# Requests for weights and residual rows kept in written order on SyncE's queue

## The chip, the cores and the metric

The kernel runs on one core of one Trainium2 chip. A core has five engines that work side by side, each through its own instructions in order: TensorE (PE in the profile; PEld are its weight loads), VectorE (DVE), ScalarE (ACT), GpSimd (POOL) and SyncE (SP). SyncE computes nothing here. It issues nearly all the transfers, and while an instruction at the head of its queue waits for a semaphore, all behind it wait too. Transfers run on 16 DMA engines. The metric is device time in microseconds; 1191.49 is the median of three runs before.

## The reference

Two decoder layers over 1024 tokens of width 1024. Each layer projects its input once into a main part, memory queries and two gates; makes a main result and a cross-attention into 256 memory tokens; gates both; multiplies them by W_out; adds the scaled input and normalises.

```python
def mixer_sublayer(x, mem, w_in, w_mem_kv, w_out, main_fn):
    h = x @ w_in
    u_main = h[..., :D_MAIN]
    q_mem = h[..., D_MAIN:D_MIX]
    g_main = h[..., D_MIX:D_MIX + D_MAIN]
    g_mem = h[..., D_MIX + D_MAIN:]
    y_main = main_fn(u_main)
    y_mem = memory_attention(q_mem, mem, w_mem_kv)
    y = jnp.concatenate([y_main * jax.nn.silu(g_main), y_mem * jax.nn.silu(g_mem)], axis=-1)
    return y @ w_out
...
        x = layer_norm(ALPHA * x + y, ln_g[layer], ln_b[layer])
```

The main result of layer 0 is a causal pooling; that of layer 1 is a causal attention of 16 heads of width 64, with a forget bias that is added to the logits. Its keys and values come from one projection of layer 0's output.

## The kernel before

Every product is made of two or three matmuls of narrower numbers: a weight or an activation is split into a high and a low half, and the halves are multiplied crosswise.

*Slabs.* `slab` projects onto 128 columns: two pieces of weights of 128 x 512, 48 matmuls of 512 columns, two accumulators, each evacuated when it is full. In layer 1 the slabs of keys (`k_units`), queries (`q_units`), values (`v_units`) and gates (`gate_units`) are generators. The attention sweep (`fox`) goes through 16 heads, two to a pair, and 8 tiles of 128 queries to a head, from the longest row of keys to the shortest, and between its own matmuls it pumps matmuls out of a list of such generators (`Fill`). The slabs of pair p+1 are filled in while pair p is attended to: k, then q, then v, and with pairs 0, 2, 4 and 7 gate slabs as well. So the order of TensorE is written out by hand there (`tc.manual_schedule`).

*How a slab of the fill gets its weights.* While `low[0]` is set, both pieces come in one transfer of 512 KB into a tile of the tag "B" (ten buffers), line 332. Then GpSimd scales a piece (L176), makes its high half (L193) and its low half (L178). The generator yields after the request and after each split, and `Fill.pump` takes these three steps of the slab that is second in the list: the request as soon as the slab ahead of it has become the first, the splits when fewer than 30 and 16 of its 48 matmuls are left. The head pair's k slab is stepped at set tiles instead (i = 2, 5 and 6 of the second head).

*Other work on SyncE in the sweep.* `turn` issues a transpose of a tile's probabilities (L1081), with the values' matmuls (L1090) six tiles later; `move` copies halves of a finished k or q slab to other partitions (L909), three transfers of which the third overwrites what the first read; `forget_rows` loads the bias of a head (L1009); `values_of` transposes a v slab (L823); results are stored (L1119) and late gates load and store them again (L1126, L1131). GpSimd also makes the masks of the diagonal (L1002), which VectorE reads with the logits (L1028).

*W_out.* `OutProj` holds 24 pieces of W_out to a layer. In layer 1, `fetch_two` asks for them two at a time during the last head pair and after it (L557), `split` takes them in order some tiles later. `rest` then goes through four blocks of 256 rows and three chunks of W_out's rows: it loads gated results (L634), splits them, multiplies (L599) and, after a block's last chunk, calls `norm`, which loads the residual rows (L655), adds (L659), normalises and stores (L673).

*What sets the order of the rest.* Outside what is written by hand, a planner orders each engine's instructions by their place in the program and by when it thinks that they are ready and their buffer is free. An instruction without inputs, such as a load of weights, can so be issued long before the place at which it is written. `tc.keep_in_program_order` gives an instruction an order-only edge to the instruction written just before it on the same engine; it is not issued before that one. It adds no wait for that one's end, and later instructions are not held behind it by it.

Of the kernel before, what the change touches and what calls it, by code (L numbers as in the profile page):

```python
# [18 lines left out]
P = 128  # L19
# [53 lines left out]
def run(units):  # L73
    for _ in units:
        pass
# [3 lines left out]
def trunk_kernel(ctx, tc, x, xT, memT, win, wk, wv0, wv, wmk, wmv, wout, poolw, pscale, lng, lnb, bforget, out):  # L79
# [5 lines left out]
    nc = tc.nc  # L85
# [18 lines left out]
    def sb(shape, tag, bufs, dt=F32, where=None):  # L104
        return (where or pool).tile(shape, dt, tag=tag, name=nm(tag), bufs=bufs)

    def ps(shape, tag, bufs):
        return psum.tile(shape, F32, tag=tag, name=nm(tag), bufs=bufs)

    def G(shape=(P, S), dt=F32):  # L110
        return sb(list(shape), "G", 4, dt)

    def T(shape=(P, S), dt=F32R):
        return sb(list(shape), "T", 6, dt)
# [10 lines left out]
    def tiny(n, dt=F32):  # L125
        return small.tile([P, n], dt, tag=f"s{n}{dt}", name=nm("s"), bufs=4 if n < 12 else 2)
# [53 lines left out]
    def parts_of(make, shape):  # L180
        return Split(make(shape), make([shape[0], 2] + list(shape[1:]), BF16))
# [7 lines left out]
    def three(a, b):  # L189
        return (a.hi, b.hi), (a.top, b.lo), (a.lo, b.hi if isinstance(a, Wide) else b.top)  # L190
# [18 lines left out]
    def split_w(src_dram, shape, sc=None, r=None, pin=lambda ins: ins):  # L209
        if r is None:  # L210
            r = raw(shape)
            nc.sync.dma_start(r, src_dram)
        if sc is not None:
            to = half_of(wt, shape)
            if low[0]:
                gp_scaled_hi_lo(to, r, sc)
            else:
                scaled_hi_lo(to, r, sc, pin)
            return to
        to = parts_of(wt, shape)  # L220
        (gp_hi_lo if low[0] else hi_lo)(to, r)
        return to
# [102 lines left out]
    def slab(pieces_dram, X, evac, banks=("pj", 2), g=0):  # L325

        arrived = isinstance(pieces_dram, list)
        sc = sws[g] if isinstance(X, Half) else None
        both = (None, None)
        if low[0]:  # L330
            wide = roomy[0]([P, 2, 4, P])
            nc.sync.dma_start(wide, pieces_dram.rearrange("c p k m -> p c k m"))
            both = wide[:, 0], wide[:, 1]
            yield 0
        ws = list(pieces_dram) if arrived else [split_w(pieces_dram[0], [P, 4, P], sc, both[0])]
        if low[0]:
            yield 0
            ws.append(split_w(pieces_dram[1], [P, 4, P], sc, both[1]))
            yield 0
        accs = {}  # L340
        high, low_top = (0,), (1, 2)
        if sc is not None:
            order = [(n, pc, (0, 1, 2)) for n in range(2) for pc in range(2)]
        elif arrived:
            order = [(n, pc, part) for pc in range(2) for n, part in ((0, high), (1, high), (1, low_top), (0, low_top))]
        else:
            order = [(0, pc, part) for part in (high, low_top) for pc in range(2)]
            order += [(1, pc, part) for part in (low_top, high) for pc in range(2)]
        seen = {0: 0, 1: 0}
        for n, pc, part in order:  # L350
            if len(ws) <= pc:
                ws.append(split_w(pieces_dram[pc], [P, 4, P], sc, both[pc]))
            if n not in accs:
                accs[n] = ps([P, NH], *banks)
            for i in part:
                a, b = three(ws[pc], X)[i]
                for k in range(4):
                    seen[n] += 1
                    nc.tensor.matmul(  # L359
                        accs[n], a[:, k, :], b[:, pc * 4 + k, n * NH : (n + 1) * NH],  # L360
                        start=seen[n] == 1, stop=seen[n] == 3 * KT,
                    )
                    if seeing[0]:
                        seeing[1] += 1
                        if seeing[1] % 8 == 0:
                            look_ahead()
                    if seen[n] == 3 * KT:
                        evac(slice(n * NH, (n + 1) * NH), accs[n])
                    yield NH
# [174 lines left out]
    class OutProj:  # L544
# [8 lines left out]
        def fetch_two(self, land):  # L553

            n = self.n + len(self.raws)
            for j, to in enumerate(land):
                nc.sync.dma_start(to, wout[self.l, n // 2 % 2, 2 * self.KKS[n // 4] + j])  # L557
                self.raws.append(to)

        def fetch(self, upto):  # L560
# [54 lines left out]
        def rest(self, resid, X, dst):  # L615
            order = [(sp, c) for sp in range(ST // 2) for c in (2, 0, 1)]
            accs, splits, gb = {}, [24], []
            if self.accs:
                accs[0], order[:6], splits = self.accs, [(0, 0), (1, 2), (0, 1), (1, 0), (1, 1)], [16, 24]
            if X is not None:  # L620
                self.split(splits.pop())

            def loads():

                for v in (lng, lnb):
                    t = sb([P, D], "P", 4)
                    nc.sync.dma_start(t, v[self.l].partition_broadcast(P))
                    gb.append(t)

            for sp, c in order:  # L630
                if c == 2:
                    accs[sp] = self.open((("T", 2), ("T", 2), ("L", 3), ("O", 1))) if 0 in accs and sp == 1 else self.open()
                src, ys = T([P, 4, 2 * P], F32), parts_of(T, [P, 4, 2 * P])
                nc.sync.dma_start(src, self.yd[c, :, :, sp * 2 * P : (sp + 1) * 2 * P])  # L634
                hi_lo(ys, src)
                if splits:
                    self.split(splits.pop(0), X is None)
                if not gb and not splits:
                    loads()
                run(self.products(accs[sp], c, ys, X is None and sp == ST // 2 - 1 and c == 1))  # L640
                if X is not None and (sp, c) == (0, 0):
                    scale_of_norm(gb)
                if X is not None and c == 0 and sp:
                    scales_of_weights(sp - 1)
                if X is not None and c == 0 and sp in (1, 2):
                    keep(sp - 1)
                if c == 1:
                    norm(sp, accs.pop(sp), gb, resid, X, dst)

    def norm(sp, accs, gb, resid, X, dst):  # L650
        for a in range(2):
            s = 2 * sp + a
            rows = slice(s * P, (s + 1) * P)
            z = G()
            nc.sync.dma_start(z, resid[rows, :])  # L655
            stats = tiny(12)
            for nh in range(2):
                zn = z[:, nh * NH : (nh + 1) * NH]
                nc.vector.scalar_tensor_tensor(zn, zn, ALPHA, accs[a][nh], ALU.mult, ALU.add)  # L659
                nc.vector.bn_stats(stats[:, 6 * nh : 6 * nh + 6], zn)  # L660
            mv, v, sd, r, t = tiny(2), tiny(1), tiny(1), tiny(1), tiny(1)
            nc.vector.bn_aggr(mv, stats.rearrange("p (a b) -> p a b", a=2))
            nc.vector.tensor_scalar(v, mv[:, 1:2], LN_EPS, None, ALU.add)
            nc.scalar.activation(sd, v, AF.Sqrt)
            nc.vector.reciprocal(r, sd)
            nc.vector.tensor_scalar(t, r, r, v, ALU.mult, ALU.mult)
            nc.vector.tensor_scalar(t, t, -0.5, 1.5, ALU.mult, ALU.add)
            nc.vector.tensor_tensor(r, r, t, ALU.mult)
            for cols in (slice(0, NH), slice(NH, D)) if s == ST - 1 else (slice(0, D),):
                nc.vector.scalar_tensor_tensor(z[:, cols], z[:, cols], mv[:, 0:1], gb[0][:, cols], ALU.subtract, ALU.mult)  # L670
            for cols in (slice(0, NH), slice(NH, D)) if s == ST - 1 else (slice(0, D),):
                nc.vector.scalar_tensor_tensor(z[:, cols], z[:, cols], r, gb[1][:, cols], ALU.mult, ALU.add)  # L672
                nc.sync.dma_start(dst[rows, cols], z[:, cols])  # L673
            if X is not None:
                two = Half(*(lines[0][:, 9 + 2 * (s % 3) + e, :] for e in range(2)))
                scaled_hi_lo(two, z, sx)
                for to, half in ((X.hi, two.hi), (X.lo, two.lo)):
                    nc.sync.dma_start_transpose(to[:, :, rows], half)
# [5 lines left out]
    X = parts_of(stream, [P, KT, S])  # L684
# [110 lines left out]
    X = X1  # L795
# [501 lines left out]
```

## Time and profile before

| | us |
|---|---|
| median of 3 runs (lowest, highest) | 1191.49 (1191.08, 1192.35) |
| the profiled execution | 1193.08 |
| its span | 1191.4 |
| TensorE busy | 1166.9 |
| VectorE busy | 782.7 |
| ScalarE busy | 684.8 |
| GpSimd busy | 286.0 |

The span runs from the first to the last instruction; the execution's own time holds a little more. Rows of a timeline give the start and the duration in microseconds, the engine (SPq is SyncE's queue, where the duration is that of issuing), the line, the operation, what is written and read, and a count where equal instructions are merged; in brackets stand the idle time of the engine before it and what ended it. Rows of stages give the stretch and its length, then busy time and count for TensorE, its weight loads, VectorE, ScalarE and GpSimd, then the granted TensorE clock, the busy share of the DMA engines and GB/s. Layer 0 ends at about 480 us, the attention sweep fills 645 to 1050, and the output projection of layer 1 with the norms fills the rest.

### The profile page before, as it was taken

Reading aid. Unit: us, or ns where it says so; the run is one execution under the profiler, and the core shown is the slowest. Engines: PE = TensorE matmul, PEld = TensorE weight load, DVE = VectorE, ACT = ScalarE, POOL = GpSimd, SP = SyncE. Lnnn points to the kernel's source line nnn. Section 1 sums busy time; section 2 is a strip of 40 time slices with the busy share of each in tenths; the row PEclk is TensorE's granted clock in tenths of the full one; section 3 lists DMA queues with packets and bytes.
Section 4 is the critical chain, followed back from the end, with each engine's and each line's share of the span. In section 5 each row is a group of like instructions: output and inputs, shape, how many; then the busy total and the mean of one; then the engine's idle time right before and its main releaser. Section 6 shows DMA issues by size and latency. Waiting matters only on the chain. (4 is left out here: it accounts for less than half of the span.)

```text
span 1191.4 us, 19838 instructions
## 1 busy us (share of the span) xinstructions
PE 1166.9 (98%) x6941; PEld 672.7 (56%) x6941; DVE 782.7 (66%) x1840; ACT 684.8 (57%) x1512; POOL 286.0 (24%) x437
## 2 busy tenths in 40 slices
PE   8999999999999999999999999999999999999996
PEld 5566766555555557556664555555555545455553
DVE  5754675555765557357645888778877788884654
ACT  6578875875663234467421776666766677674210
POOL 3322001310000000000002454555555444760000
PEclk9999999999999999999999999999999999999999
DMA  7576656854385555445734789989996899965430
GB/s 261 176 247 198 165 103 208 255 173 148 101 283 160 152 137 134 110 142 108 197 124 113 172 181 221 187 174 204 191 211 147 168 197 205 238 166 169 175 108 35
DMA packets 286196, 203.88 MB, mean 171 GB/s; under 512 B 224913, under 2 KB 238353, under 8 KB 286097
## 3 DMA queue, kind: packets, MB, share of 16 engines
q1 hardware_dynamic: 279696, 181.59, 61.2%
q0 software_dynamic: 6400, 21.04, 5.5%
q8 instruction: 54, 0.88, 0.3%
q14 instruction: 46, 0.37, 0.1%
HBM read 116.01 MB, written 22.61 MB: 116 GB/s over the span
## 5 line engine op out<-in xcount | busy, mean ns | idle before, releaser
L359 PE MATMUL pj<-A,w 128*128 128x512 f16 (+2 forms) x2896 | 662.9, 383 | 1.9 <-ACT MK L200 0.6
L359 PEld LDWEIGHTS <-w 128*128 128x128 f16 (+1 forms) x2560 | 245.6, 98 | 278.3 <-issue 9.5
L1036 ACT ACTIVATE T<-MK,s 128x512 f32<-128x512 f32 x192 | 111.2, 579 | 65.9 <-DVE s L1028 48.8
L1065 DVE SCALAR_TENSOR_TENSOR P<-T,s,P 128x512 f16<-128x512 f32 x192 | 112.0, 613 | 39.1 <-ACT P L1064 37.9
L1064 ACT ACTIVATE P<-T,s 128x512 f16<-128x512 f32 x192 | 102.9, 576 | 53.3 <-issue 28.9
L599 PEld LDWEIGHTS <-T 128*128 128x128 bf16 x736 | 70.6, 98 | 89.2 <-issue 4.4
L1002 POOL TENSOR_SCALAR_AFFINE_SELECT raw<-R 128x256 f32<-128x256 f32 (+3 forms) x128 | 59.8, 468 | 185.5 <-DVE s L1028 102.0
L323 PE MATMUL L<-A 128*128 128x512 f16 (+3 forms) x384 | 84.8, 326 | 5.5 <-DVE s L1028 5.4
L199 DVE TENSOR_TENSOR w<-raw,w 128x512 bf16<-128x512 f32 x74 | 52.0, 703 | 53.9 <-ACT w L198 37.9
L885 POOL MEMSET G<- 128x128 f32 x1 | 0.2, 204 | 334.9 <-DVE V L541 334.9
L359 PEld LDWEIGHTS pj<-A,w 128*128 128x128 f32 x352 | 65.2, 188 | 17.0 <-ACT w L198 1.3
L199 DVE TENSOR_TENSOR T<-T,T 128x1024 bf16<-128x1024 f32 x23 | 28.1, 1220 | 70.2 <-PE pj L599 38.2
L323 PEld LDWEIGHTS <-A 128*128 128x128 f16 x384 | 37.3, 98 | 48.9 <-issue 7.6
L178 POOL TENSOR_TENSOR w<-B,w 128x512 f16<-128x512 f32 x54 | 63.2, 1172 | 4.0
L198 ACT CAST T<-T 128x1024 fp32r<-128x1024 f32 x23 | 24.1, 1047 | 64.0 <-DMA T<-y1d 34.4
L198 ACT CAST w<-raw 128x512 fp32r<-128x512 f32 x76 | 46.8, 615 | 23.9 <-DMA raw<-in_win_dram 10.6
L1090 PEld LDWEIGHTS <-V 128*64 128x64 f16 (+1 forms) x1152 | 50.6, 104 | 13.0 <-issue 5.6
L1090 PE MATMUL O<-T,V 128*64 128x128 f16 (+1 forms) x1152 | 57.5, 221 | 0.1
L599 PE MATMUL pj<-B,T 128*128 128x512 bf16 (+1 forms) x192 | 53.1, 385 | 0.0
L1028 DVE CUSTOM_DVE_ANT_0 MK<-L,R,scales 128x512 f32<-128x512 f32 x64 | 45.3, 708 | 9.7 <-PE L L323 9.4
L200 ACT CAST w<-raw 128x512 bf16<-128x512 f32 x78 | 48.2, 618 | 3.3 <-PE pj L359 1.9
L599 PE MATMUL L<-B,T 128*128 128x512 bf16 (+1 forms) x168 | 47.3, 394 | 0.0
(289 smaller groups left out, 1850.0 us busy)
## 6 DMA issues: line engine op xcount, KB each, us to landing
raw<-in_win_dram SPq DMA_DIRECT2D x66, 256.0 KB, 3.4
W<-in_win_dram POOLq DMA_DIRECT2D x48, 256.0 KB, 4.2
R<-cumd SPq DMA_DIRECT2D x16, 512.0 KB, 4.6
B<-in_win_dram SPq DMA_DIRECT2D x15, 512.0 KB, 4.9
y0d<-Y SPq DMA_DIRECT2D x12, 512.0 KB, 4.0
raw<-in_wout_dram SPq DMA_DIRECT2D x24, 256.0 KB, 2.7
T<-y0d SPq DMA_DIRECT2D x12, 512.0 KB, 4.2
A<-A SPq DMA_DIRECT2D x24, 256.0 KB, 4.0
```

Source lines behind the costliest of these rows:

```text
L178: pin(nc.gpsimd.tensor_tensor(to.lo, src, to.hi, ALU.subtract))
L198: pin(nc.scalar.copy(to.hi, src))
L199: pin(nc.vector.tensor_tensor(to.lo, src, to.hi.bitcast(F32), ALU.subtract))
L200: pin((top or nc.scalar.copy)(to.top, src))
L323: nc.tensor.matmul(acc, a, b, start=i == 0, stop=i == len(terms) - 1)
L359: nc.tensor.matmul(accs[n], a[:, k, :], b[:, pc * 4 + k, n * NH : (n + 1) * NH], start=seen[n] == 1, stop=seen[n] == 3 * KT,)
L599: nc.tensor.matmul(accs[a][nh], y, w, start=kt == 8 and i == 0, stop=kt == 7 and i == 2,)
L1002: tc.keep_in_program_order(nc.gpsimd.affine_select(C[:, :w], R[:, lo:up], [[-1, w]], ALU.is_ge, -NEG, base=w - P, channel_multiplier=1,))
L1036: nc.scalar.activation(e, p[:, lo:up], AF.Exp, bias=top, scale=-1.0, accum_out=sums[:, n, hd % 2, i : i + 1],)
L1064: nc.scalar.activation(pair[:, lo:up], e, AF.Copy, scale=r)
L1065: nc.vector.scalar_tensor_tensor(pair[:, L + lo : L + up], e, r, pair[:, lo:up], ALU.mult, ALU.subtract)
L1090: nc.tensor.matmul(acc[rows, (i % 4) * P : (i % 4) * P + P], v[:, b, 2 * j : 2 * j + (1 if e else 2), :].rearrange("p e d -> p (e d)"), pt ...
```

## The change

Three kinds of transfers on SyncE's queue are given the order-only edge: the weights of the fill (L332), the pieces of W_out that `fetch_two` asks for (L557), and the residual rows. The residual rows also move in the program: both rows of a block are requested ahead of the products of its last chunk, by a new function `rows_of`, instead of one at a time in `norm`. The instructions stay the same in number, size and kind.

```diff
             wide = roomy[0]([P, 2, 4, P])
-            nc.sync.dma_start(wide, pieces_dram.rearrange("c p k m -> p c k m"))
+            tc.keep_in_program_order(nc.sync.dma_start(wide, pieces_dram.rearrange("c p k m -> p c k m")))
             both = wide[:, 0], wide[:, 1]
...
             for j, to in enumerate(land):
-                nc.sync.dma_start(to, wout[self.l, n // 2 % 2, 2 * self.KKS[n // 4] + j])
+                tc.keep_in_program_order(nc.sync.dma_start(to, wout[self.l, n // 2 % 2, 2 * self.KKS[n // 4] + j]))
                 self.raws.append(to)
...
+                if c == 1:
+                    zs = rows_of(resid, sp)
                 run(self.products(accs[sp], c, ys, X is None and sp == ST // 2 - 1 and c == 1))
...
                 if c == 1:
-                    norm(sp, accs.pop(sp), gb, resid, X, dst)
-
-    def norm(sp, accs, gb, resid, X, dst):
+                    norm(sp, accs.pop(sp), gb, zs, X, dst)
+
+    def rows_of(resid, sp):
+        zs = [G() for _ in range(2)]
+        for a, z in enumerate(zs):
+            tc.keep_in_program_order(nc.sync.dma_start(z, resid[(2 * sp + a) * P : (2 * sp + a + 1) * P, :]))
+        return zs
+
+    def norm(sp, accs, gb, zs, X, dst):
         for a in range(2):
             s = 2 * sp + a
             rows = slice(s * P, (s + 1) * P)
-            z = G()
-            nc.sync.dma_start(z, resid[rows, :])
+            z = zs[a]
             stats = tiny(12)
```

## The prediction

> **What bounds the kernel now.** I read the page first, then the stages of the attention sweep, then SyncE's queue there, then what stands right behind the requests that the change moves.
>
> ```profile
> span 1191.4 us, 19838 instructions
> PE 1166.9 (98%) x6941; PEld 672.7 (56%) x6941; DVE 782.7 (66%) x1840; ACT 684.8 (57%) x1512; POOL 286.0 (24%) x437
> ```
>
> ```profile
> 700.00:800.00 100.00, 99.23 (x684) 51.51 (x683) 77.48 (x228) 68.17 (x164) 52.16 (x79) 1.00 0.95 198
> 800.00:900.00 100.00, 99.56 (x697) 52.47 (x692) 77.48 (x226) 68.23 (x162) 50.96 (x77) 1.00 0.95 193
> 900.00:1000.00 100.00, 98.18 (x743) 53.05 (x742) 79.52 (x238) 70.16 (x171) 48.98 (x76) 1.00 0.88 179
> 1000.00:1050.00 50.00, 47.63 (x303) 24.16 (x302) 42.71 (x106) 36.65 (x84) 33.60 (x47) 1.00 0.96 220
> ```
>
> The profiled execution took 1193.08 us, 1.7 more than its span and 1.6 more than the median of the runs, 1191.49. TensorE (PE) is the bound: in the four stages of the sweep it idles 0.8, 0.4, 1.8 and 2.4 us at full granted clock, 5.4 us of 350. So the change can take next to nothing away there, and TensorE's order is written out by hand: a matmul whose weights are late stops everything behind it. The DMA engines are 88 to 96% busy.
>
> **Fill weights now: asked for long ahead.**
>
> ```profile
> 579.09 0.53 SPq L332 DMA_DIRECT2D B<-in_wk_dram  x1
> 579.72 0.42 SPq L332 DMA_DIRECT2D B<-in_win_dram  x1
> 580.23 0.42 SPq L332 DMA_DIRECT2D B<-in_wv_dram  x1
> 588.73 0.38 SPq L332 DMA_DIRECT2D B<-in_wk_dram  x1
> ```
>
> ```profile
> DMA to landing us min/median/max: 3.8/4.9/9.4
> ```
>
> The second fence is line 332's row (27 requests). The first shows the k, q and v weights of head pair 2, and the k weights of pair 3, requested before the sweep begins. Pair 2's v slab runs near 727: its request stands about 147 us ahead. Nothing orders these requests except a free "B" buffer.
>
> **The change, part 1: the 27 fill weights (L332).** Pinned, each one goes behind the SyncE instruction written just before it. In the code a slab's request is made when the slab before it in the fill begins. For a v slab that is right behind the k slab's three moves (L909); the third overwrites what the first read, so it waits for the first to land.
>
> ```profile
> 715.37 1.34 SPq L909 DMA_DIRECT2D A<-A  x2
> 721.32 0.46 SPq L909 DMA_DIRECT2D A<-A  x1
> 768.34 0.53 SPq L909 DMA_DIRECT2D A<-A  x1
> 825.30 0.53 SPq L909 DMA_DIRECT2D A<-A  x1
> 869.69 0.52 SPq L909 DMA_DIRECT2D A<-A  x1
> 926.00 0.53 SPq L909 DMA_DIRECT2D A<-A  x1
> 973.58 0.53 SPq L909 DMA_DIRECT2D A<-A  x1
> ```
>
> The last six rows are that third move for pairs 2 to 7. Then the weights must land and GpSimd (POOL) must scale them and make the high half:
>
> ```profile
> 714.69 0.69 POOL L176 TENSOR_SCALAR B<-B,scales 128x512 f32<-128x512 f32 x1
> 715.47 0.62 POOL L193 TENSOR_SCALAR w<-B 128x512 f16<-128x512 f32 x1
> 716.17 1.15 POOL L178 TENSOR_TENSOR w<-B,w 128x512 f16<-128x512 f32 x1
> ```
>
> From 714.69 to 716.09 is 1.4 us to the first usable half. So a v slab can start at: end of the third move + 0.1 + 4.9 (median landing) + 1.4 = end + 6.4. It is wanted when the q slab before it ends. The q slab's second evacuation shows that from above, since it cannot start before the q slab's last matmul:
>
> ```profile
> 727.61 0.60 ACT L912 ACTIVATE A<-pj 128x512 f16<-128x512 f32 x1
> 767.18 0.60 ACT L912 ACTIVATE A<-pj 128x512 f16<-128x512 f32 x1
> 830.21 0.60 ACT L912 ACTIVATE A<-pj 128x512 f16<-128x512 f32 x1
> 869.77 0.60 ACT L912 ACTIVATE A<-pj 128x512 f16<-128x512 f32 x1
> 932.81 0.60 ACT L912 ACTIVATE A<-pj 128x512 f16<-128x512 f32 x1
> 980.32 0.60 ACT L912 ACTIVATE A<-pj 128x512 f16<-128x512 f32 x1
> ```
>
> Late by pair: 2: 721.78 + 6.4 - 727.61 = 0.6. 3: 768.87 + 6.4 - 767.18 = 8.1. 4: 825.83 + 6.4 - 830.21 = 2.0. 5: 870.21 + 6.4 - 869.77 = 6.8. 6: 926.53 + 6.4 - 932.81 = 0.1. 7: 974.11 + 6.4 - 980.32 = 0.2. Sum 17.8. Pairs 3 and 5 are worst because gate slabs share their fill, so the q slab passes in fewer steps. In the other four ScalarE may pick the evacuation up as much as a microsecond after the matmul; I add 0.8 for each and take **21 us**. Each stop moves the whole hand-written order, so stops add up. Ends: with the fastest landing, 3.8, the terms are 7.0, 0.9 and 5.7 and the sum 13.6; with the slowest, 9.4, each grows by 4.5 to about 48. I stay at the median, as most requests will queue on engines as busy as now.
>
> The k and q slabs get their weights behind a transpose (L1081) of the running step, three or more steps before use, and I cost them at nothing: their cover is the stretch from the first split to the matmul, some 12 us by the rows of pair 2's v slab (714.69 to 727.61). Gate slabs of pairs 2 and 4 come right behind a stopped v slab, which gives them the time. If that cover goes, each costs 1 to 2 us.
>
> [...]
>
> **Part 2: what a stop draws with it.**
>
> ```profile
> 603.04 4.23 PE L848 MATMUL pj<-MK,A 128*128 128x272 f16 x21 [2.06 <-DVE G L857]
> 603.00:606.40 3.40, 3.36 (x15) 2.25 (x16) 0.61 (x3) 0.28 (x1) 0.00 (x0) 0.50 0.61 239
> 1034.07 0.38 PE L323 MATMUL L<-A 128*128 128x256 f16 x2 [2.05 <-DVE s L1028]
> ```
>
> After an idle of 2.06 us the granted clock was 0.50 for 3.4 us, 1.7 us of work lost; after one of 2.05 us, in the stage whose row shows 1.00, none was. So zero to 1.7 us for each stop over 2 us. I take two, for the long ones: **3 us**; ends 0 and 10.
>
> [...]
>
> GpSimd waits for the weights too, and the diagonal masks (L1002) share its order, with VectorE's logits behind them.
>
> ```profile
> POOL raw L1002 <- DVE s L1028: 102.0, 50, 4.1
> ```
>
> Masks now wait 102 us for VectorE to free their buffers, so they run ahead as far as the four buffers let them. A stopped split can use that up. I take **2 us**, between 0 and 2 for each of six slabs.
>
> **Part 3: pieces of W_out (L557).** All are split some steps after they are asked for. The last eight are written after the transpose at 1053.71 and now must be issued behind it, close ahead of the first loads of the output projection:
>
> ```profile
> 1051.38 2.01 SPq L557 DMA_DIRECT2D A<-in_wout_dram  x3
> 1053.71 1.21 SPq L1081 DMA_TRANSPOSE T<-P  x1
> 1057.02 0.33 SPq L1131 DMA_DIRECT2D y1d<-R  x1
> 1057.44 1.47 SPq L634 DMA_DIRECT2D T<-y1d  x2
> 1062.45 1.05 ACT L198 CAST T<-T 128x1024 fp32r<-128x1024 f32 x1 [3.96 <-DMA T<-y1d]
> 1064.59 0.60 PE L599 MATMUL L<-B,T 128*128 128x512 bf16 x2
> ```
>
> That load has no slack: ScalarE waits 3.96 us for it, and TensorE takes the split tile at 1064.59. Three requests take 2.01 us, so eight take 5.4 from 1054.92, to 1060.3, and 2 MB lie ahead on the engines: 0 (issued after the load) to 6 us. I take **2**.
>
> **Part 4: residual rows (L655).** Both rows of a block are asked for behind the load of its last chunk (L634), before the products instead of after. They take two of four "G" buffers, whose stores left a block ago.
>
> ```profile
> 1136.80 7.94 SPq L634 DMA_DIRECT2D T<-y1d  x2
> 1156.04 0.33 SPq L655 DMA_DIRECT2D G<-x  x1
> 1174.65 0.69 DVE L659 SCALAR_TENSOR_TENSOR G<-G,L 128x512 f32<-128x512 f32 x1 [16.69 <-PE L L599]
> ```
>
> The second L634 ends at 1144.74; both rows would land near 1151, and VectorE wants the first at 1174.65, when it is released by TensorE and not by a load. Cost nothing; covered by 23 us of products, and the other seven blocks are built alike. If that cover went, the norm at the end would wait a landing, some 5 us.
>
> **Sum:** 1193.1 + 21 + 3 + 2 + 2 = 1221 for an execution like the profiled one, 1.6 less by the median: **1220 us**.
>
> **Rivals.** *Larger.* Landings nearer 7 us, the clock halved at most stops, masks late: 21 + 6 x 2 = 33, + 8 + 6 + 4 = 51, 1243. For it: DMA engines 95% busy, longest landing 9.4. Against: median 4.9 under the same load. *Small.* The third moves come sooner, since the eight early requests no longer lie among them, and only pairs 3 and 5 stop, each some 4 us: 8, 1200. *No change.* GpSimd's lead hides everything, or the pins do not bind, each being an edge to one instruction only: if that one floats, so does the request. 1191 to 1193. Against: the instruction ahead of a v request is a move that needs the k slab's own results. *Faster.* The requests at 579 to 590 no longer load the engines before the sweep. It decides if the gap of 2.06 us at 603.04 and the half clock behind it are due to them: 3.8 less, 1188. Against: the row names VectorE's L857 as releaser, not a load.
>
> **How the numbers follow.** Chances: forecast (1207 to 1234) 0.60, larger 0.17, small 0.13, no change 0.05, faster 0.05. A tenth each way is left out: 1202 to 1245. 0.2% is 2.4 us, about what a measurement of this kernel tells from nothing; the first three cases end slower: 0.90, same 0.05, faster 0.05.
>
> **What would show it.** L332 spread over 640 to 1030, with none in a burst at 579 to 590; L176 with idle time released by "DMA B<-in_wv_dram"; TensorE idle before L359 at six places, longest at pairs 3 and 5, released by POOL's L193; busy PE in 700 to 1000 down by about 20 us; windows at clock 0.50; unchanged times from 1064 to the end. I am wrong if TensorE's gaps in the sweep stay near 5 us, or if they stand before L323 (masks) or L1090 (transposes) instead.

## The result and the profile after

The changed kernel takes 1230.39 us (median of 4 runs, 1229.67 to 1232.43); the kernel before took 1191.28 beside it (4 runs). The ratio is 1.0332, with a 95% interval of 1.0319 to 1.0345: 39 us slower, 10 more than forecast and inside the range. The profiled execution took 1229.67 us.

The page of the changed kernel, its span and engines, and then the stages of the sweep (columns as in the prediction):

```profile
span 1227.5 us, 19760 instructions
PE 1178.5 (96%) x6894; PEld 675.3 (55%) x6941; DVE 781.0 (64%) x1840; ACT 684.9 (56%) x1512; POOL 283.3 (23%) x437
```

```profile
700.00:800.00 100.00, 88.77 (x596) 45.43 (x595) 67.64 (x197) 60.12 (x145) 46.44 (x70) 0.95 0.85 178
800.00:900.00 100.00, 92.09 (x633) 47.32 (x632) 66.95 (x198) 59.12 (x143) 40.90 (x64) 0.95 0.77 168
900.00:1000.00 100.00, 96.93 (x689) 51.05 (x688) 75.32 (x223) 65.78 (x159) 44.71 (x70) 0.98 0.87 179
1000.00:1100.00 100.00, 90.82 (x606) 47.25 (x605) 73.58 (x188) 64.55 (x144) 57.76 (x82) 0.97 0.96 233
```

The work of the other engines is the same; TensorE idles and, in part, runs slower. Its busy time even rises by 11.6 us, 1166.9 to 1178.5, although it does the same matmuls: those at a lower granted clock take longer, at half clock twice as long (0.86 us for two, 0.43 at full clock, below). (47 matmuls have no record in this trace; their weight loads, 6941, are all there.) So two things have to be found, the stops and the clock.

The stops of the sweep, from TensorE's timeline of the changed kernel:

```profile
725.16 2.31 PE L359 MATMUL pj<-A,w 128*128 128x512 f16 x5 [3.50 <-POOL w L193]
775.52 4.02 PE L359 MATMUL pj<-A,w 128*128 128x512 f16 x9 [7.20 <-POOL w L193]
840.68 1.68 PE L359 MATMUL pj<-A,w 128*128 128x512 f16 x4 [1.91 <-POOL w L193]
889.56 1.89 PE L359 MATMUL pj<-A,w 128*128 128x512 f16 x4 [5.55 <-POOL w L193]
956.44 1.82 PE L359 MATMUL pj<-A,w 128*128 128x512 f16 x5 [2.63 <-POOL w L193]
1007.30 1.92 PE L359 MATMUL pj<-A,w 128*128 128x512 f16 x6 [2.07 <-POOL w L193]
```

Six stops, one for each v slab of pairs 2 to 7, each ended by GpSimd's high half of the weights: 22.9 us together. The chain of one of them, pair 3, on SyncE's queue and GpSimd (the lines of the moves are now L916, those of `turn` L1088):

```profile
761.65 6.22 SPq L1088 DMA_TRANSPOSE T<-P  x2
767.98 0.53 SPq L916 DMA_DIRECT2D A<-A  x1
768.56 0.58 SPq L332 DMA_DIRECT2D B<-in_wv_dram  x1
773.51 1.36 POOL L176 TENSOR_SCALAR B<-B,scales 128x512 f32<-128x512 f32 x2 [7.30 <-DMA B<-in_wv_dram]
774.85 1.20 POOL L193 TENSOR_SCALAR w<-B 128x512 f16<-128x512 f32 x2
```

The third move, the request right behind it, a landing, GpSimd idle for 7.30 us until the weights are there, then the high half and, at 775.52, TensorE. GpSimd scales both pieces before it makes the first high half, so TensorE starts 2.0 us after GpSimd does, where the prediction took 1.4; all six slabs go this way. The landing, the time from a request's issue to the arrival of its data, is the one that was assumed; the row of line 332 says (least, median, most):

```profile
DMA to landing us min/median/max: 4.0/4.9/7.3
```

The clock: these are all windows of the sweep and of what follows it with the granted clock at half, up to the last norm, in the changed kernel.

```profile
724.90:728.30 3.40, 3.14 (x8) 1.19 (x9) 0.00 (x0) 0.00 (x0) 3.40 (x6) 0.50 1.07 229
772.70:779.50 6.80, 3.98 (x10) 1.49 (x11) 0.00 (x0) 0.67 (x2) 5.33 (x7) 0.50 0.67 187
840.90:844.30 3.40, 3.40 (x10) 1.19 (x9) 1.07 (x4) 0.72 (x4) 3.40 (x6) 0.50 0.90 227
888.70:895.50 6.80, 5.94 (x14) 2.11 (x15) 0.00 (x0) 0.35 (x1) 4.18 (x6) 0.50 0.52 143
957.00:960.40 3.40, 3.40 (x10) 1.18 (x8) 0.00 (x1) 0.00 (x0) 3.40 (x5) 0.50 1.10 247
1008.20:1011.60 3.40, 3.40 (x10) 1.19 (x9) 0.34 (x3) 0.00 (x0) 2.94 (x5) 0.50 1.18 233
1096.90:1103.70 6.80, 5.32 (x13) 1.94 (x14) 5.33 (x6) 6.75 (x11) 2.39 (x2) 0.50 0.08 34
sum 34.00, PE 28.59 PEld 10.29 DVE 6.73 ACT 8.48 POOL 25.04; mean PE 4.08 PEld 1.47 DVE 0.96 ACT 1.21 POOL 3.58
```

Each of the six stops is followed by such a window, the two long ones by a double one, and a seventh stands at the start of the output projection. TensorE was busy for 28.59 us in them. In the last one its timeline shows two matmuls of the output projection start every 0.85 or 0.86 us from 1099.20 to 1103.47, and behind it, at full clock, every 0.43 or 0.44 us from 1104.48 to 1105.78. At half the time for the same work, 14.3 us went there, an estimate from these rows, 11.6 of them in the sweep.

The start of the output projection, in the timeline:

```profile
1083.79 2.37 SPq L557 DMA_DIRECT2D A<-in_wout_dram  x3
1086.72 3.10 SPq L557 DMA_DIRECT2D A<-in_wout_dram  x5
1089.92 1.42 SPq L634 DMA_DIRECT2D T<-y1d  x2
1096.33 1.04 ACT L198 CAST T<-T 128x1024 fp32r<-128x1024 f32 x1 [9.65 <-DMA T<-y1d]
1098.38 1.03 PE L599 MATMUL L<-B,T 128*128 128x512 bf16 x2 [5.41 <-ACT T L200]
```

The last eight pieces of W_out, three and five, are issued ahead of the first load of gated results, ScalarE waits for that load for 9.65 us where it was 3.96, and TensorE stops for 5.41.

One thing went the other way. The first logits of the sweep, by line 323's row up to 660 us, in the changed kernel and then in the kernel before:

```profile
L323 PE MATMUL L<-A x20: 272/352/379, 644.4 to 658.6; 128*128 128x512 f16 x10, 128*128 128x384 f16 x6, 128*128 128x256 f16 x4
```

```profile
L323 PE MATMUL L<-A x16: 272/353/380, 649.3 to 658.4; 128*128 128x512 f16 x8, 128*128 128x384 f16 x4, 128*128 128x256 f16 x4
```

The sweep starts 4.9 us sooner. TensorE's stop of 2.06 us at 603.04, and the window at half clock behind it (1.7), are gone; the rest is an earlier start.

The account between the two profiled executions: -4.9 before the sweep, +22.9 of stops, +11.6 of clock in the sweep, -2.7 at the masks (TensorE's idle time before line 323 fell from 5.5 to 2.8), +5.4 and +2.7 at the output projection. That is 35.0 of a difference of 36.1 between the spans.

### The profile page after: what moved, and what is told of

It is laid out like the page before. It is cut to its first block, busy times and chain, and to the rows that moved or that the text cites. A ratio compares the mean times of both kernels' runs of the same rounds, so it can differ in the third digit from the quotient of the medians.

```text
span 1227.5 us, 19760 instructions
## 1 busy us (share of the span) xinstructions
PE 1178.5 (96%) x6894; PEld 675.3 (55%) x6941; DVE 781.0 (64%) x1840; ACT 684.9 (56%) x1512; POOL 283.3 (23%) x437
## 5 line engine op out<-in xcount | busy, mean ns | idle before, releaser
L359 PE MATMUL pj<-A,w 128*128 128x512 f16 (+2 forms) x2875 | 673.4, 387 | 25.9 <-POOL w L193 23.2
L176 POOL TENSOR_SCALAR B<-B,scales 128x512 f32<-128x512 f32 x54 | 37.2, 691 | 66.9 <-DMA B<-in_win_dram 33.8
```

The costliest lines, as they stand in the source:

```text
L359: nc.tensor.matmul(accs[n], a[:, k, :], b[:, pc * 4 + k, n * NH : (n + 1) * NH], start=seen[n] == 1, stop=seen[n] == 3 * KT,)
```

## The experiments

Each was timed against the kernel before on the same chip. "Theory" is that of the prediction, sharpened by the two traces: the weights of a v slab leave behind the third move of the k slab, too late by a landing; the last eight pieces of W_out delay the first load of the output projection; the residual rows cost nothing.

**One part at a time.** The weights of the fill alone: the edge at lines 557 and 655 taken away again, `rows_of` too.

```diff
-                tc.keep_in_program_order(nc.sync.dma_start(to, wout[self.l, n // 2 % 2, 2 * self.KKS[n // 4] + j]))
+                nc.sync.dma_start(to, wout[self.l, n // 2 % 2, 2 * self.KKS[n // 4] + j])
...
-                if c == 1:
-                    zs = rows_of(resid, sp)
```

> Only the weights of the fill are pinned; pieces of W_out and residual rows stay as before. Theory (late v weights stop TensorE six times and halve its clock; the eight pinned pieces of W_out delay the output projection's first load by themselves): the sweep's loss of about 33 us stays, the stop of 5.4 us before the output projection and its half clock, 8 us together, go: 1221 to 1224. Rival (the stop before the output projection is a consequence of the late sweep, not of W_out's pins): 1229 to 1231.

Measured: 1229.08 us, ratio 1.0319 (1.0288 to 1.0351). The six stops are there (2.27, 7.33, 2.33, 5.75, 2.82, 2.62 us) and the one at the output projection is gone, as the theory says. But the time did not fall by those 8 us. The timeline of this run shows what stands in their place:

```profile
1050.50 7.54 SPq L557 DMA_DIRECT2D A<-in_wout_dram  x3
1060.48 0.43 SPq L332 DMA_DIRECT2D B<-in_win_dram  x1
1067.06 0.69 POOL L176 TENSOR_SCALAR B<-B,scales 128x512 f32<-128x512 f32 x1 [5.94 <-DMA B<-in_win_dram]
1068.50 2.55 PE L359 MATMUL pj<-A,w 128*128 128x512 f16 x11 [1.67 <-POOL w L193]
1073.65 0.82 PE L359 MATMUL pj<-A,w 128*128 128x512 f16 x3 [2.06 <-POOL w L193]
```

```profile
SPq L557 <- POOL MK L193: 6.1, 1, 6.1
```

Three free requests of W_out occupy SyncE's queue for 7.54 us, where five took 3.10 in the changed kernel. By the row of this run's waits on that queue, 6.1 us of it are one request waiting for GpSimd to split an earlier piece. The weights of the last gate slab, which may no longer float ahead, are issued behind them, and TensorE stops for 1.67 and 2.06 us, the second with a window at half clock. So the expected time was missed because what one pinned kind of request costs depends on how the others are ordered. The sum of the medians doesn't show it: weights alone 3.2% slower, W_out alone 0.3% (below), all together 3.3%, each with an interval of 0.1 to 0.3% to both sides.

The pieces of W_out alone, in the kernel before:

```diff
-                nc.sync.dma_start(to, wout[self.l, n // 2 % 2, 2 * self.KKS[n // 4] + j])
+                tc.keep_in_program_order(nc.sync.dma_start(to, wout[self.l, n // 2 % 2, 2 * self.KKS[n // 4] + j]))
```

> Only the pieces of W_out are pinned. Theory: no stops in the sweep; the eight last requests stand ahead of the output projection's first load, TensorE stops 3 to 6 us there and loses up to 2.7 us to the clock: 1195 to 1200. Rival (a consequence of the late sweep): 1190 to 1193.

Measured: 1196.00 us, ratio 1.0034 (1.0020 to 1.0049), with a stop of 5.27 us at the output projection and slow matmuls behind it: two take 1.03 to 1.06 us there, 0.60 ahead of the stop, as at half and at full clock in the changed kernel. The theory holds: a few microseconds, all at that place but for two stops of 1.45 us before late gate slabs.

The residual rows alone, in the kernel before:

```diff
+                if c == 1:
+                    zs = rows_of(resid, sp)
...
-            z = G()
-            nc.sync.dma_start(z, resid[rows, :])
+            z = zs[a]
```

> Only the residual rows are moved ahead of the products and pinned. Theory: rows are wanted 23 us after they land, nothing changes: 1190 to 1193. Rival (two rows held for longer in four buffers, or two loads more ahead of the next chunk's load, delay the norms or the products): 1194 or more.

Measured: 1190.10 us, ratio 0.9991 (0.9976 to 1.0006): no change, as expected.

**Taking the lateness away.** All three kinds stay pinned, but each slab of the fill, the v slabs among them, makes its request one slab sooner, when the slab two places ahead in the list begins:

```diff
         while self.due > 0 and self.units:
+            if len(self.units) > 2 and self.units[2][2] == 3:
+                next(self.units[2][0])
+                self.units[2][2] -= 1
...
+            units = slab(wv[p - 2], X, lambda cols, acc: value_halves(two, cols.start // NH, acc), g=2)
+            yield next(units)
             two = MK([P, ST, 2, P], F16)
```

> All pins as in the changed kernel, but the fill asks for the weights of the third slab of its list too, so v weights are asked for one slab sooner, ahead of the k slab's moves. Theory: the six stops and their half clock go (33 us), the stop before the output projection stays (8 us), and the 4.9 us that the changed kernel gains before the sweep stay: 1193 to 1198. Rival (stops come from GpSimd's order of masks and splits, or from the order that the planner gives the other engines): 1215 or more.

Measured: 1197.61 us, ratio 1.0042 (1.0027 to 1.0058). 33 of the 39 us are gone, and with them all the windows at half clock of the sweep. TensorE's groups in this run:

```profile
L362 PE MATMUL pj<-A,w 128*128 128x512 f16 (+2 forms) x2875 | 662.4, 383 | 6.6 <-POOL w L196 4.1 <-ACT MK L203 0.6 <-DVE Y L379 0.3
L602 PE MATMUL L<-B,T 128*128 128x512 bf16 (+1 forms) x165 | 48.0, 401 | 5.1 <-ACT T L203 4.9
```

Against the changed kernel (673.4 us at 387 ns, 25.9 of idle time, 23.2 for GpSimd's L193) the slabs' matmuls are busy for 11 us less, which is the clock, and wait 19 us less. What is left is the stop at the output projection, 4.94, and two late gate slabs. So the order itself costs next to nothing in the sweep; the lead that it takes away does.

**What is it that makes the request late?** By the code it is the third move, which overwrites what the two before it read and so waits for both to land. Here the request is made once the k slab's last matmul is out, ahead of the third move, which is issued after it:

```diff
         while self.due > 0 and self.units:
+            if len(self.units) > 2 and self.units[2][2] == 3 and self.units[0][1] <= 0:
+                next(self.units[2][0])
+                self.units[2][2] -= 1
...
-                    move((odd, high64, own, high64), (odd, low64, own, high64), (own, high64, own, low64))
+                    move((odd, high64, own, high64), (odd, low64, own, high64))
 
             yield from slab(ready.get(("k", p), wk[p]), X, evac, g=1)
+            move((own, high64, own, low64))
...
+            units = slab(wv[p - 2], X, lambda cols, acc: value_halves(two, cols.start // NH, acc), g=2)
+            yield next(units)
             two = MK([P, ST, 2, P], F16)
```

> The changed kernel with one order changed: a v slab's weights are asked for once the last matmul of the k slab ahead of it is out, and the third move of that k slab is issued behind the request, not ahead of it. By theory the lateness comes from the third move's own wait for the first move's landing, which stands ahead of the request on SyncE's queue: the request then leaves some 4 to 7 us sooner (at pair 3 near 761.6 us where it was 768.56), the six stops before the value slabs go to under 2 us together at most, and with them the clock windows at half; the stop at the output projection stays at some 5 us: 1196 to 1203 us. The rival is that the request is late because it is made at all so near its use, whichever move stands ahead: the landing of some 5 us then still ends behind the need at three pairs or more, and the time is 1210 us or more.

Measured: 1201.57 us, ratio 1.0084 (1.0068 to 1.0099), inside the theory's interval. At pair 3 the timeline has

```profile
755.90 1.92 SPq L335 DMA_DIRECT2D B<-in_wv_dram  x1
762.63 0.46 SPq L919 DMA_DIRECT2D A<-A  x1
763.74 1.37 POOL L179 TENSOR_SCALAR B<-B,scales 128x512 f32<-128x512 f32 x2 [5.38 <-DMA B<-in_wv_dram]
765.75 5.94 PE L362 MATMUL pj<-A,w 128*128 128x512 f16 x14 [4.23 <-POOL w L196]
```

The request now leaves 6.7 us ahead of the third move (755.90 and 762.63), four of the six stops are gone with their windows at half clock, pair 5 keeps 1.10 us, and pair 3 keeps 4.23 with a window of 6.8 us: there the request takes 1.92 us to issue, and GpSimd starts 7.8 us behind its start, where the median landing is 4.9. "Under 2 us together" was therefore wrong, 5.3 remain; but the main price of the change was indeed some 7 us behind a transfer that stood ahead in the queue.

What fills those 7 us the experiment doesn't part, but the traces show it. In this run SyncE waits 3.4 us at pair 3's third move for the landing of the moves before it:

```profile
SPq L919 <- DMA A<-A: 3.4, 1, 3.4
```

In the changed kernel the two moves of pair 3, issued from 759.83 on, landed 5.9 and 5.4 us after their issue, the later at 766.35. Two transposes stand between them and the third move (761.65, 6.22 us above), and their issue ends 1.5 us after that landing; at pairs 4 to 7 it ends 0.9 to 1.5 us after it, at pair 2 before it. So the landing sets most of the delay, and the transposes add the rest at five of the six pairs. The prediction took the third moves' times from the trace before, so its sum held both; its words name the landing alone.

**Is it the landing?** The other way to make the weights come sooner, with the request left where the change puts it, is a smaller transfer. Two requests of 256 KB in place of one of 512 KB:

```diff
-            tc.keep_in_program_order(nc.sync.dma_start(wide, pieces_dram.rearrange("c p k m -> p c k m")))
             both = wide[:, 0], wide[:, 1]
+            for pc in range(2):
+                tc.keep_in_program_order(nc.sync.dma_start(both[pc], pieces_dram[pc]))
```

> The changed kernel with each slab's weights asked for in two requests of 256 KB, one for each piece. The first lands some 1.5 us sooner, so each of the six stops is some 1.5 us shorter: 23 us become 14. Theory (the clock is halved for 3.4 us only after a stop of about 1.9 us or more inside one window): three or four windows of 1.7 us go as well: 1213 to 1218. Rival (any stop costs a half window): 1220 to 1223. If the first piece lands no sooner: 1229 to 1232.

Measured: 1211.78 us, ratio 1.0162 (1.0138 to 1.0187). The landing row of these requests and the longest stop:

```profile
DMA to landing us min/median/max: 2.9/3.7/6.6
```

```profile
768.33 2.21 PE L360 MATMUL pj<-A,w 128*128 128x512 f16 x5 [4.70 <-POOL w L193]
```

Median landing 1.2 us shorter, the six stops 11.0 us together instead of 22.9 (0.77, 4.70, 0.99, 2.84, 0.78, 0.88), and only the two long ones are followed by a half-clock window, of 3.4 us each. The time fell a little more than expected: four stops, now of 0.77 to 0.99 us, drew no half-clock window, as the theory had it, and the two double windows became single ones besides.

**The output projection.** Everything free as before, except the pieces of W_out, of which only the last eight are left free:

```diff
-        def fetch_two(self, land):
+        def fetch_two(self, land, pin=tc.keep_in_program_order):
...
-                nc.sync.dma_start(to, wout[self.l, n // 2 % 2, 2 * self.KKS[n // 4] + j])
+                pin(nc.sync.dma_start(to, wout[self.l, n // 2 % 2, 2 * self.KKS[n // 4] + j]))
...
-                            out_proj.fetch_two(two_lines(4 + 2 * i))
+                            out_proj.fetch_two(two_lines(4 + 2 * i), lambda ins: ins)
```

> Only pieces of W_out pinned, and of them not the last eight. Theory (the last eight are what stands ahead of the output projection's first load): the stop of 5.3 us there and its half clock go: 1189 to 1192. Rival (the earlier pieces, in written order, delay the late gates or the load): 1194 to 1198, as with all of them pinned.

Measured: 1191.10 us, ratio 0.9988 (0.9973 to 1.0004). The stop is down to 0.77:

```profile
1061.67 0.60 PE L599 MATMUL L<-B,T 128*128 128x512 bf16 x2 [0.77 <-ACT T L200]
```

So it is those last requests, held behind the last transposes and ahead of the load, that cost the microseconds of the W_out part; the order of the other pieces costs nothing that can be measured.

**Is there a gain to be kept?** The first stop of the kernel before, at 603.04, is gone in the changed kernel. With the v weights asked for sooner, and the late gates' requests, W_out and the rows free again, only that gain should be left. The edits that ask sooner are those above; the others are:

```diff
+            ask = nc.sync.dma_start(wide, pieces_dram.rearrange("c p k m -> p c k m"))
+            if not loose[0]:
+                tc.keep_in_program_order(ask)
...
+            loose[0] = True
+            first = next(units)
+            loose[0] = False
```

> Weights of k, q, v and early gate slabs pinned but asked for one slab sooner; weights of the late gates, pieces of W_out and residual rows as before. Theory (stops come from weights asked for too late, and from W_out's requests ahead of the first load): neither stop is left, and with no burst before the sweep the gap near 603 goes as well: 1187 to 1191. Rival (order on the queue costs time in itself, by waits between the requests): 1194 or more.

Measured: 1191.97 us, ratio 0.9994 (0.9980 to 1.0007). No stop before a slab of the sweep is over 0.8 us, and there is none near 600, yet no gain that can be told from none: the expected 1187 to 1191 was missed. A likely reason is in the other traces. The part before the sweep is the same in the kernel before and in the runs with W_out, the rows, or the first pieces of W_out changed, and there the stop near 600 was 0.60, 0.56 and 0.46 us, without a half-clock window. The profiled execution of the kernel before, with 2.06 us and a window, had the dear case; it lay 1.8 us above its median.

**What is that stop?** Its row names VectorE's L857 as releaser. But the stores of layer 1's V to memory (`y1d<-V`) free the buffers that the value projection writes, and those landed later when the seven requests of 579 to 590 lay beside them. The landing row of these four stores, in the kernel before and in the changed one:

```profile
DMA to landing us min/median/max: 7.6/8.8/9.8
```

```profile
DMA to landing us min/median/max: 2.6/2.6/3.8
```

And in the kernel before, at the stop, ScalarE, which goes ahead of VectorE there, was released by one of them:

```profile
602.24 0.45 ACT L855 ACTIVATE V<-pj 128x128 f16<-128x128 f32 x2 [0.92 <-DMA y1d<-V]
```

To test it, four loads of 512 KB, whose data is read by nobody, were put ahead of the stores in the kernel that has no such stop:

```diff
+        if l:
+            for f in range(4):
+                tc.keep_in_program_order(nc.sync.dma_start(roomy[0]([P, 2, 4, P]), win[1, f].rearrange("c p k m -> p c k m")))
```

> The same with four more loads of 512 KB, whose data nobody reads, pinned ahead of the four stores of gated memory results before the sweep. Theory (a burst of weights ahead of these stores delays their landing from 2.6 us to 8 or more, and the value projection waits for the buffers that they read): TensorE's gap near 600 is back, 0.6 to 2.1 us with half clock for the longer, so 0.6 to 4 us more than without the loads. Rival (the gap comes from another thing in that stretch): the same time as without, within 0.5 us, stores landing in under 4 us.

Measured: 1191.53 us, ratio 0.9995 (0.9980 to 1.0010). The stores landed after 5.9 us (median), and TensorE didn't stop: the expectation was missed. The first landed 3.3 us behind the start of the value projection (603.1 and 599.8); in the traces that have the stop, of 0.46 to 2.06 us, it was 4.4 us or more. So the burst was doubled, to eight loads (`range(8)`):

> The kernel without stops (value weights asked for sooner, the rest free again) with eight extra loads of 512 KB ahead of the stores of the second layer's V, where the run before had four; the data of these loads is read by nobody. By theory (a store that lands late holds the buffers of the value projection) the first store now lands 4.5 us or more behind the start of the value projection's first matmul, TensorE stops near 600 us for 0.5 to 3 us, and the time is 1 to 5 us more than that of the kernel before. The rival is that the stop of the kernel before comes from VectorE's own work, as its row names VectorE: no stop, and 1190 to 1193 us.

Measured: 1200.14 us, ratio 1.0058 (1.0035 to 1.0081). The landing row of the stores, and the timeline:

```profile
DMA to landing us min/median/max: 8.8/12.1/13.3
```

```profile
602.67 0.45 ACT L863 ACTIVATE V<-pj 128x128 f16<-128x128 f32 x2 [8.99 <-DMA y1d<-V]
602.99 0.49 DVE L864 SCALAR_TENSOR_TENSOR V<-pj,V 128x128 f16<-128x128 f32 x2 [6.05 <-ACT V L863]
604.12 0.22 DVE L865 SCALAR_TENSOR_TENSOR G<-pj,scales,bfb 128x16 f32<-128x16 f32 x1
604.40 7.83 PE L856 MATMUL pj<-MK,A 128*128 128x272 f16 x42 [5.49 <-DVE G L865]
```

TensorE's row still names VectorE. VectorE waited for ScalarE (6.05), and ScalarE for the store (8.99). So a burst of requests ahead of those stores does stop the value projection, here for 5.49 us with 6.8 us at half clock behind it; the price, 0.6% or some 7 us, was above the expected 1 to 5, by the length of the stop.

## Why the prediction was right, and where it was not

*Where TensorE stops, and why.* Right: six stops before v slabs, longest at pairs 3 and 5, released by GpSimd's L193, GpSimd idle for the weights, the requests spread over the sweep. That what stands on the queue up to the third move makes the request late is shown by issuing that move behind the request, and that the lead is the price by asking sooner.

*Their size: 21 us.* Measured 22.9. Term by term: pair 2, 0.6 + 0.8 forecast, 3.50; pair 3, 8.1 and 7.20; pair 4, 2.8 and 1.91; pair 5, 6.8 and 5.55; pair 6, 0.9 and 2.63; pair 7, 1.0 and 2.07. The long ones were forecast a microsecond too long, three of the short ones one to two too short and pair 4 0.9 too long; the sum came out by errors that cancel in part. One error is in the term of 1.4 us from GpSimd's start to the first usable half, read off a slab whose pieces were split one by one: 2.0 in all six here, since both pieces are scaled first. "I stay at the median" for the landing was right for the sum; pair 2 had the longest, 7.3 us, and that is most of its 3.50.

*The clock: 3 us.* This is the term that failed: 14.3 us, beyond its own end of 10. The step was "I take two, for the long ones". All six stops drew a window, and so did the one at the output projection, and the long ones a double one. The forecast had a row on each side, 2.06 us with the clock halved and 2.05 us without; it set them against each other by length, and length alone did not tell them apart (below). The rival "Larger" had "the clock halved at most stops", and was right in that.

*The masks: 2 us.* None: TensorE's idle time before line 323 fell from 5.5 to 2.8 us. Stops of TensorE may give GpSimd and VectorE time to catch up; this was not tested.

*W_out: 2 us.* The place and the cause were right, the size not: 5.4, near its upper end of 6, and 2.7 of clock with it, for which no term stood.

*Residual rows: 0.* Right, by the run with the rows alone.

*Not in the sum.* 4.9 us were gained ahead of the sweep. It is what the rival "Faster" named, and the ground given against it, that the row names VectorE, did not hold: the chain behind that row leads to a store. Alone it is worth little in a median, as the run without stops shows. "Unchanged times from 1064 to the end" contradicted the forecast's own 2 us for W_out, and was wrong by it.

Between the profiled executions 28 us were forecast and 36.6 measured. Of the 8.6 that were missing, +11.3 are the clock (14.3 for 3), +3.4 W_out, +1.9 the stops, -2 and -2.7 the masks, -4.9 the stretch ahead of the sweep: +7.0; the other 1.6 are not resolved.

## What to carry to other kernels

A load that the scheduler has let float long ahead is covered by its lead, not by its place in the text; before it is pinned, find the instruction that it is pinned behind, what that one waits for and what else stands ahead on the queue, and compare the time left with one landing under the load of that stage. If the order is wanted all the same, move the request in the program by one stage: here that gave back 33 of 39 us. Price a stop of TensorE with the clock that follows it: in the run with two requests the stops of 0.8 to 1.0 us cost their length alone, while the changed kernel's six of 1.9 to 7.2 us, 22.9 together, cost 11.6 more by the clock.

## What the runs showed of the hardware

*Length alone did not tell whether half clock followed a stop.* The seven stretches at half clock from 724.9 us on in the changed kernel are 3.4 or 6.8 us long. Counted from the first, the others begin 14, 34, 48, 68, 83 and 109 times 3.413 us later (the last at 1096.9, 372.0 us behind 724.9). I divided the traces of the two kernels into lengths of 3.413 us, counted from such a stretch. From 595 to 1150 us TensorE idled 2.02 us or more in the length just ahead of each of these seven and of the one at 603.0 in the kernel before, and 1.29 us at most in every other length at full clock. Of the pair of rows in the prediction, the stop of 2.06 us at 603.04 fell with 2.02 into one length; that of 2.05 us at 1034.07 fell into two, 1.05 and 1.00, and no half clock followed.

In the run with the weights alone a longer stop, too, was followed by full clock:

```profile
724.66 2.12 PE L359 MATMUL pj<-A,w 128*128 128x512 f16 x9 [2.27 <-POOL w L193]
```

```profile
724.00:727.00 3.00, 2.34 (x11) 1.03 (x12) 1.60 (x5) 1.25 (x5) 3.00 (x5) 1.00 0.85 201
```

Counted back from that run's half-clock stretch at 771.2, a length ended near 723.4, so the 2.27 us fell into two, 1.1 and 1.2; this is an estimate by the same count. The three stretches of 6.8 us in the changed kernel had 0.84 us or more of idle time in their first half, the four of 3.4 us 0.28 at most. No run varies the place of a stop by itself, so more than these counts was not shown.

*A releaser is the last link only.* The stop at 603 was put down to VectorE, in the profile and in the prediction; two links further back stood a store that landed late beside a burst of loads, in 7.6 to 9.8 us where it took 2.6 to 3.8 without.
